# Parked operands written out one per neighbourhood head and fetched in the order of use, the last neighbourhood head with both score pairs first, and the two halves of a key block copied in one go

## The chip, the cores and the metric

The kernel runs on one core of a Trainium2 chip. The metric is the device time of one execution in microseconds (us); less is better. The kernel computes one denoising step of a small two-layer backbone. Three runs of the kernel before gave 1475.26, 1476.01 and 1476.55 us.

## The reference, cut to what matters

There are 512 latent tokens and 128 context ("prompt") tokens, so most operands are 640 columns wide, and 128 cached context tokens. Layer 0 mixes tokens by two kinds of heads, eight each; layer 1 by grouped-query attention; each layer ends in a SwiGLU feed-forward block. The change is in the mixer of layer 0:

```python
def even_mixer_latent(h, c_ckv, c_krope, c_nk, c_nv, w_in, q_norm, w_uq, kv_norm, w_ukv, rpb, w_out, cos, sin):
    q, ckv, krope, nq, nk, nv = even_project(h, w_in, q_norm, w_uq, kv_norm, w_ukv)
    q = jnp.concatenate([q[..., :MLA_NOPE_DIM], apply_rope(q[..., MLA_NOPE_DIM:], cos, sin)], axis=-1)
    krope = apply_rope(krope[:, :, None, :], cos, sin)[:, :, 0, :]
    k_lat, v_lat = mla_expand(ckv, w_ukv, krope)          # keys and values out of the 256-wide ckv
    k_ctx, v_ctx = mla_expand(c_ckv, w_ukv, c_krope)      # the same for the cached context
    a_mla = attend_blocked(q, cat(k_lat, k_ctx), cat(v_lat, v_ctx), MLA_SCALE)
    a_na = neighbourhood_attention(nq, nk, nv, c_nk, c_nv, rpb)
    return jnp.concatenate([a_mla, a_na], axis=-1) @ w_out
```

The MLA heads use `cq` (the 256-wide compressed query), `ckv` (256 wide) and `krope` (a rotary key of 32). All of it is computed in float32.

## The kernel before

**Arithmetic.** A float32 product is emulated on TensorE: each operand is split into a high part (`...h`, rounded to the fp32r type) and a low part (`...l`, the rest), and three matmuls (high by high, low by high, high by low) are added. A split costs two instructions: a copy on ScalarE (ACT) that makes the high part, and a subtraction on VectorE (DVE) that makes the low one. Weights arrive by DMA as float32 in one of a few `raw` buffers (`load`) and are split by `unit`, for the weights `wm0` to `wm3` with the subtraction on GpSimd (POOL).

**Stages.** After the input projection (which leaves `ckv`, `cq` and `kr`, the rotary key, unsplit on the chip) come the neighbourhood heads 0 to 7 ("NA"), from 113 to 218 us, then the MLA heads, then the output projection and the rest. Only the NA heads and the MLA heads are touched by the change.

**Parking.** The buffers that hold the split `ckv`, `cq` and `kr` for MLA are not free while NA runs. So `park` splits an operand in temporary buffers (three buffers of 640 columns, `tmp`, tiles `pt...h` and `pt...l`) and writes both parts to DRAM (tiles `pk...`). `latents`, `unpark` and `k_rope` fetch them back: `ck`, `ckp` (columns 512 to 640 and the cached context), `cq0`, `cq1` and the rotary rows of the key tiles `kT`. All these DMAs are issued from one queue, SyncE (SP), which also issues the loads of the weights and of the tables `gt` and `tq`. There are five parking steps, one written ahead of each of the heads 1 to 5 (`PARK_AT`).

**What sets the order.** The program lists its pieces by hand: `sequence` runs the pieces of a head in the order of a string. The strings for the heads 1 to 7 are in `NA_ORDER`: `s0`, `s1` are the two pairs of score blocks, `sp` the prompt's scores, `t0` to `t2` transposes and `v0` to `v2` the weighted values of the head before (the head's tail), `pt` and `pv` the same for the prompt, `q..` projection pieces of the next pair of heads, `m..` pieces of the modulation (weights `mraw`, `mraww`), and in head 7 `k0`, `k1` the first key block of MLA and `u0`, `u1` its first query. A second string orders the tail of head 7 beside the first two value blocks of MLA, `b0` and `b1`. The scheduler that builds the program places the instructions of the other engines into their queues; `tc.issue_after(x)` tells it that what is written inside stands behind `x`, but only on the engine of `x`. Each piece is issued after the last TensorE instruction before it, and so is a parking step by `after(PE.last, ...)`: this orders TensorE and nothing on ACT, DVE or SP, where the queue alone counts. Every engine works off its own queue strictly in order.

**Keys and queries of MLA.** `k_pieces` makes the key block of a pair of heads in two pieces: `mk..0` (512 columns) and `mk..1` (256). When a piece's matmuls are done, `k_set` copies it into the tiles of the even head (partitions 0 to 63, `kT..`) and of the odd head (64 to 127, `kT..` or `kTo`), once per head: ACT makes the high part, DVE the low part. `q_pieces` multiplies a query by a rotary table on DVE (`mqt`, table `tq0` for head 0 and `tq` for the others), and splits it. `mla_w(p)` loads and splits the weight `wm{p}`. `half_sum` adds the two halves of an attention result (ACT copies the upper half to `nhs` or `mhs`, DVE adds into `oN`).

Of the kernel before, what the change touches and what calls it, by code (L numbers as in the profile page):

```python
# [51 lines left out]
def body(ctx, tc, xT, vecs, crow, wm0, wm0g1, wm0g, wm1, wA, wNV, wNA, wMK, wMV, wOA, wGQ, wGK, wGV, wOC,  # L52
# [108 lines left out]


    def load(src, n, name):
        raw = rawp.tile([P, 1024], F32, tag="raw", name=name)
        nc.sync.dma_start(raw[:, :n], src)
        return raw[:, :n]

    def unit(src, n, name, lo="v", pool=None, bufs=3):
# [5 lines left out]
        (V if lo == "v" else G).tensor_tensor(lw, raw, f(hi), ALU.subtract)
# [236 lines left out]
    def half_sum(dsts, ps, n, pool, name):  # L411

        t = pool.tile([64, 512], F32, tag="hs", bufs=1, name=name)
        S.activation(t[:, :n], ps[64:128, :n], AF.Copy)
        for dst, a, b in dsts:
            V.tensor_tensor(dst, ps[0:64, a:b], t[:, a:b], ALU.add)
# [364 lines left out]
    def na_scores(h, bm, pts):  # L781
# [5 lines left out]
        def piece(jj):  # L787
            banks = [bank(f"ns{h}_{jj}{i}", "y") for i in range(2)]
            for j in (2 * jj, 2 * jj + 1):
                pss = banks[j % 2]  # L790
                k0, cq = P * PLACE[j][0], slice(P * j, P * j + P)
                PE.matmul(pss[:, 0:384], qh[:, cq], ks[:, k0:k0 + 384], start=True, stop=False)
                PE.matmul(pss[:, 0:384], ql[:, cq], ks[:, k0:k0 + 384], start=False, stop=True)
            for j in (2 * jj, 2 * jj + 1):
# [1 line left out]
                V.tensor_tensor_reduce(pt, banks[j % 2][:, :384], bm[:, (0, 1, 1, 2)[j], :], -1.0, 3.0e38, ALU.add, ALU.min,
                                       mm[:, j:j + 1])
# [90 lines left out]

    def k_set(r, rows, parts, src, p=0):

        jobs = []
        for c in parts:
            c0, c1 = KPART[c]
            o = c0 - KPART[parts[0]][0]
            h, l = [(prompt if c == 2 else main_[:, c0:c1])[rows] for main_, prompt in k_tiles(r, p)]
            jobs.append((h, l, src[rows, o:o + c1 - c0]))
# [1244 lines left out]
```

## Time and profile before

| | |
|---|---|
| runs | 1475.26, 1476.01, 1476.55 us; median 1476.01 |
| the profiled execution | 1476.62 us; its span 1474.5 us, so 2.12 us lie around it |
| TensorE (PE) busy | 1440.1 us, 98% of the span |
| VectorE (DVE), ScalarE (ACT), GpSimd (POOL) busy | 1231.4, 783.3, 175.0 us |
| granted TensorE clock | 0.996 |

All times inside an execution are counted from the start of the span. A row of the timeline gives start, duration, engine, line, operation, output and inputs, and in brackets how long the engine stood idle before it and what it waited for. Tile names have lost their numbers there, so `ns` is a score block of any NA head, `ms` of an MLA head, `mo` an MLA head's value product, `mts_0l` the low part of the transposed probabilities.

### The profile page before, as it was taken

To read this page: it belongs to the slowest core of one execution; us is meant where nothing else is said; L and a number is where in the kernel's file an instruction comes from. 1 tells how busy PE (TensorE), PEld (TensorE's weight loads), DVE (VectorE), ACT (ScalarE), POOL (GpSimd) and SP (SyncE) were. 2 spreads that over 40 slices of the span, in tenths; PEclk is the share of its full clock that TensorE was granted. 3 is DMA by queue.
4 is the path that set the end of the run, shared out by engine and by line. 5 is a ranking of instruction groups with operands and counts; after the bars stand their busy time and mean duration, and the time that the engine had idled before them with its cause. 6 is when DMAs were issued, how large, how long until landed. Compare 5 with 4: busy or idle time off the path is not lost.

```text
span 1474.5 us, 25877 instructions
## 1 busy us (share of the span) xinstructions
PE 1440.1 (98%) x9764; PEld 1390.1 (94%) x9764; DVE 1231.4 (84%) x2350; ACT 783.3 (53%) x1530; POOL 175.0 (12%) x270
## 2 busy tenths in 40 slices
PE   5999999999999999999999999999999999999997
PEld 4988888889999999999999999989999999999997
DVE  5877668877898989965997888888899898989976
ACT  5446667763755555541122666672656555555443
POOL 0037545430000000000000122220000000000000
PEclk9999999999999999999999999999999999999999
DMA  9655471026165555569764310115245555548572
GB/s 369 211 185 194 135 243 46 15 73 200 47 202 173 168 168 170 173 223 326 241 220 155 101 34 30 43 37 194 84 169 178 184 174 185 174 147 294 185 270 72
DMA packets 84884, 239.22 MB, mean 162 GB/s; under 512 B 9496, under 2 KB 15800, under 8 KB 84376
## 3 DMA queue, kind: packets, MB, share of 16 engines
q1 hardware_dynamic: 82400, 233.16, 47.2%
q10 hardware_dynamic: 1944, 3.48, 0.7%
q8 instruction: 76, 1.25, 0.4%
q0 software_dynamic: 416, 0.93, 0.2%
q14 instruction: 48, 0.39, 0.1%
HBM read 197.21 MB, written 40.33 MB: 161 GB/s over the span
## 4 chain that ended last, share of the span: by engine, by line
PE 83%; DVE 7%; ACT 4%; DMA 3%; issue 2%; DVEq 0%; ACTq 0%; POOL 0%; SPq 0%
PE fg L64 19%; PE fd L64 9%; PE fgo L64 5%; PE fo L64 5%; PE fu L64 4%; PE gq L64 3%; PE fdo L64 2%; PE gs L64 2%; PE go L64 2%; PE nk L64 1%; PE fuo L64 1%; DMA mraw<-in_wm 1%; PE gt L68 1%; PE mod L64 1%; ACT mp L1036 1%
## 5 line engine op out<-in xcount | busy, mean ns | idle before, releaser
L1708 DVE SCALAR_TENSOR_TENSOR junk<-wm,cb 128x1024 bf16<-128x1024 f32 x88 | 107.4, 1220 | 4.6 <-DMA wm<-in_wm 3.7
L64 PE MATMUL gq<-h10h,wgq 128*128 128x320 f32 x256 | 65.8, 316 | 0.0
L267 POOL TENSOR_SCALAR h10h<-h10t,gs,mods 128x320 fp32r<-128x320 f32 x4 | 3.9, 990 | 430.1 <-DVE h10t L261 427.7
L1448 ACT ACTIVATE wY<-s 128x1024 fp32r<-128x1024 f32 x38 | 40.3, 1061 | 27.4 <-PE fg L64 22.5
L1448 ACT ACTIVATE wZ<-s 128x1024 fp32r<-128x1024 f32 x38 | 40.2, 1057 | 21.1 <-PE fd L64 16.0
L1976 POOL TENSOR_TENSOR xr<-xw,fn1rs 128x320 f32<-128x320 f32 x2 | 1.7, 861 | 412.8 <-ACT fn1rs L235 412.8
L1449 DVE TENSOR_TENSOR wZ<-s,wZ 128x1024 fp32r<-128x1024 f32 x38 | 46.4, 1222 | 2.5
L1449 DVE TENSOR_TENSOR wY<-s,wY 128x1024 fp32r<-128x1024 f32 x38 | 46.3, 1220 | 0.3
L64 PEld LDWEIGHTS gq<-h10h,wgq 128*128 128x128 f32 x256 | 44.9, 189 | 0.6
L1557 DVE TENSOR_TENSOR sg<-up,sg 128x640 f32<-128x640 f32 x38 | 31.3, 823 | 15.9 <-ACT sg L1556 14.9
L1556 ACT ACTIVATE sg<-fg 128x320 f32<-128x320 f32 x38 | 16.7, 438 | 48.4 <-PE fg L64 48.4
L1578 ACT ACTIVATE p<-fd 128x320 f32<-128x320 f32 x38 | 16.6, 437 | 46.3 <-PE fd L64 46.3
L64 PE MATMUL gq<-h10l,wgq 128*128 128x320 f32 x128 | 39.4, 308 | 0.0
L1913 ACT ACTIVATE gp<-gs,gb,rq 128x640 f32<-128x640 f32 (+1 forms) x40 | 31.8, 796 | 13.2 <-DVE gb L1912 11.8
L64 PE MATMUL fg<-h01E,wW 128*128 128x320 f32 x228 | 36.6, 309 | 0.7 <-DVE g L1588 0.7
L64 PE MATMUL fg<-h01N,wZ 128*128 128x320 f32 x228 | 36.6, 309 | 0.5 <-ACT p L1576 0.5
L64 PE MATMUL fg<-h11N,wZ 128*128 128x320 f32 x228 | 36.7, 309 | 0.0
L64 PE MATMUL fg<-h01q,wX 128*128 128x320 f32 x228 | 36.7, 309 | 0.0
L64 PE MATMUL fu<-h11q,wX 128*128 128x320 f32 x228 | 36.6, 309 | 0.0
L64 PE MATMUL fd<-h01q,wZ 128*128 128x320 f32 x228 | 36.6, 309 | 0.0
L64 PE MATMUL fd<-h11q,wZ 128*128 128x320 f32 x228 | 36.6, 309 | 0.0
L64 PE MATMUL fg<-h11q,wX 128*128 128x320 f32 x228 | 36.5, 309 | 0.0
(3416 smaller groups left out, 5296.0 us busy)
## 6 DMA issues: line engine op xcount, KB each, us to landing
wm<-in_wm SPq DMA_DIRECT2D x48, 512.0 KB, 4.3
mraw<-in_wm SPq DMA_DIRECT2D x8, 1024.0 KB, 13.1
mraw<-in_wm SPq DMA_DIRECT2D x14, 512.0 KB, 4.3
wmv<-in_wm0g SPq DMA_DIRECT2D x8, 512.0 KB, 4.1
wm<-in_wm0g SPq DMA_DIRECT2D x8, 512.0 KB, 4.7
ruo<-in_wFO SPq DMA_DIRECT2D x8, 512.0 KB, 4.3
rgo<-in_wFO SPq DMA_DIRECT2D x8, 512.0 KB, 5.5
x<-in_xT SPq DMA_DIRECT2D x8, 320.0 KB, 5.6
```

What stands on the lines that cost most here:

```text
L64: cls.last = nc.tensor.matmul(*a, **k)
L68: cls.last = nc.tensor.transpose(*a, **k)
L267: G.tensor_scalar(h[:, c0:c1], t, self.gsl[:, k, 0:1], self.ml[:, self.sh + k, 0:1], ALU.mult, ALU.add)
L1036: exps[h, j] = S.activation(halves(pt), pss[:, :, :HT], AF.Exp, bias=nm, accum_out=ll[:, j:j + 1])
L1448: S.activation(h, src, AF.Copy)
L1449: V.tensor_tensor(w_, src, f(h), ALU.subtract)
L1556: last = S.activation(sg[:, 0:HT], g[:, :HT], AF.Silu, scale=-1.0)
L1557: V.tensor_tensor(sg, up, sg, ALU.mult)
L1578: S.activation(p5, b5[:, :HT], AF.Copy)
L1708: V.scalar_tensor_tensor(junk, raw, 1.0, cb[:, c, :], ALU.mult, ALU.mult, accum_out=mods[l][:, j0 + i, c:c + 1])
L1913: gexp[h, j] = S.activation(dst, src, AF.Exp, bias=nb, scale=rq[:, j:j + 1], accum_out=ll[:, j:j + 1])
L1976: G.tensor_tensor(x[k][:, c0:c1], root[1][k], nrm.rs[:, c0:c1], ALU.mult)
```

## The change

Seven edits, by the diff below.

1. Parking step h is now held behind the last exponential of head h - 1 (`nexps[h - 1, 3]`, an ACT instruction), on ACT's queue. So step 1 (`ckv0`) falls late into head 0's string, step 2 (`ckv1` and the cached context) into head 1's, step 3 (`cq0`) into head 2's, step 4 (`cq1`) into head 3's and step 5 (`kr`) into head 4's.
2. The fetches are put in the order of use on SP's queue: `latents` is held behind the load of `wm0`, the fetches of `cq` behind the load of `wmv`, the rotary rows behind the fetch of `cq1`.
3. Head 7 runs `s1` directly behind `s0`.
4. The split of `wmv` (`unit`) is cut from its load and held behind the last exponential of head 7.
5. In the tail of head 7 `b0` and `b1` stand ahead of `pt`.
6. `wm1`'s split is held behind `nhs7` (`done_with[7]`), the last ACT instruction that the values of head 7 need.
7. `k_set` copies both heads' halves in one go: all copies on ACT, then all subtractions on DVE.

```diff
-        nc.sync.dma_start(raw[:, :n], src)
+        fetched[name] = nc.sync.dma_start(raw[:, :n], src)
...
-    def unit(src, n, name, lo="v", pool=None, bufs=3):
+    def unit(src, n, name, lo="v", pool=None, bufs=3, raw=None):
-        raw = load(src, n, name + "r")
+        raw = load(src, n, name + "r") if raw is None else raw
...
-            wmk[p] = unit(wMK[p], 768, f"wm{p}", lo="g")
+            wmk[p] = after(done_with[7] if p == 1 else None, lambda: unit(wMK[p], 768, f"wm{p}", lo="g"))
...
-    def latents():
+    def latents(held):
+        with tc.issue_after(held.ins):
+            return latents_()
...
-    def k_set(r, rows, parts, src, p=0):
+    def k_set(parts, src, p):
         jobs = []
-        for c in parts:
...
+        for r in range(2):
+            rows = slice(64 * r, 64 * r + 64)
+            for c in parts:
...
         for h, l, part in jobs:
             S.activation(h, part, AF.Copy)
         for h, l, part in jobs:
             V.tensor_tensor(l, part, f(h), ALU.subtract)
...
-                for r in range(2):
-                    k_set(r, slice(64 * r, 64 * r + 64), parts, ps, p)
+                k_set(parts, ps, p)
...
-    NA_ORDER += ["s0 t0 t1 pt s1 m0 v0 t2 sp m1 v1 pv m2 v2", "s0 t0 t1 k0 s1 v0 t2 sp k1 v1 u0 v2 u1"]
+    NA_ORDER += ["s0 t0 t1 pt s1 m0 v0 t2 sp m1 v1 pv m2 v2", "s0 s1 t0 t1 k0 v0 t2 sp k1 v1 u0 v2 u1"]
...
-            after(PE.last, PARK_AT[h])
+            after(nexps[h - 1, 3], PARK_AT[h])
...
-            cqs = after(PE.last, lambda: [unpark(f"cq{u}") for u in range(2)])
+            cqs = after(fetched["wmvr"], lambda: [unpark(f"cq{u}") for u in range(2)])
...
-            lat = latents()
+            lat = latents(fetched["wm0r"])
...
-            wmv = unit(wMV, 1024, "wmv")
+            wmvr = load(wMV, 1024, "wmvr")
         if h == 7:
-            for r in range(2):
-                k_rope(r, (slice(64, 128), slice(0, 64))[r])
+            wmv = after(nexps[7, 3], lambda: unit(None, 1024, "wmv", raw=wmvr))
+            with tc.issue_after(fetched["cq1"].ins):
+                for r in range(2):
+                    k_rope(r, (slice(64, 128), slice(0, 64))[r])
...
-    sequence("t0 t1 t2 pt b0 b1 v0 v1 v2 pv", {**tail, ...})
+    sequence("t0 t1 t2 b0 b1 pt v0 v1 v2 pv", {**tail, ...})
```

**ACT at the start of NA.** `nqh` and `nk` are the high parts of the first heads' queries and keys; `np` are the exponentials of head 0. Before:

```order
L852 ACTIVATE ptckv10h<-ckvr_753 128x640
L724 ACTIVATE nqh_1021<-nq_1032 64x256
L724 ACTIVATE nqh_1022<-nq_1032 64x256
L724 ACTIVATE nqh_1021<-nq_1065 64x192
L173 ACTIVATE wnk_1191<-wnk1r 128x1024
L724 ACTIVATE nqh_1022<-nq_1065 64x192
L852 ACTIVATE ptcq00h<-cqr_594 128x640
L724 ACTIVATE nqh_1021<-nq_1065 64x128
L753 ACTIVATE nk_1030<-nk_1102 64x256
L852 ACTIVATE ptcq10h<-cqr_599 128x640
L724 ACTIVATE nqh_1022<-nq_1065 64x128
L753 ACTIVATE nk_1031<-nk_1102 64x256
```

And now, from the same copy of `nqh` on:

```order
L727 ACTIVATE nqh_1021<-nq_1032 64x256
L727 ACTIVATE nqh_1022<-nq_1032 64x256
L727 ACTIVATE nqh_1021<-nq_1065 64x192
L175 ACTIVATE wnk_1191<-wnk1r 128x1024
L727 ACTIVATE nqh_1022<-nq_1065 64x192
L727 ACTIVATE nqh_1021<-nq_1065 64x128
L756 ACTIVATE nk_1030<-nk_1102 64x256
L727 ACTIVATE nqh_1022<-nq_1065 64x128
L756 ACTIVATE nk_1031<-nk_1102 64x256
L747 ACTIVATE nkf_1162<-nk_1137 128x128
```

The copies for `ckv1`, `cq0` and `cq1` (`ptckv10h`, `ptcq00h`, `ptcq10h`) no longer stand among the copies of the first queries and keys.

**DVE late in head 2's string, around 146 us.** `nql` are low parts of the queries of heads 4 and 5, `oN` the sum of head 1's values, `npp0ptl` the low part of the first pair's transposed prompt probabilities. Before:

```order
L392 RECIPROCAL nr_3r<-nl_1548 128x1
L725 SCALAR_TENSOR_TENSOR nql_1564<-nq_1584,nqh_1562 64x64
L725 SCALAR_TENSOR_TENSOR nql_1565<-nq_1584,nqh_1563 64x64
L725 SCALAR_TENSOR_TENSOR nql_1564<-nq_1584,nqh_1562 64x256
L725 SCALAR_TENSOR_TENSOR nql_1565<-nq_1584,nqh_1563 64x256
L416 TENSOR_TENSOR oN_1177<-no_1639,nhs_1698 64x448
L416 TENSOR_TENSOR oN_1177<-no_1639,nhs_1698 64x64
L392 RECIPROCAL npp1r0r<-npp1l_1656 128x1
L405 TENSOR_TENSOR npp0ptl<-npp0t,npp0pth 128x256
```

And now:

```order
L394 RECIPROCAL nr_3r<-nl_1548 128x1
L728 SCALAR_TENSOR_TENSOR nql_1564<-nq_1584,nqh_1562 64x64
L856 TENSOR_TENSOR ptcq00l<-cqr_594,ptcq00h 128x640
L728 SCALAR_TENSOR_TENSOR nql_1565<-nq_1584,nqh_1563 64x64
L728 SCALAR_TENSOR_TENSOR nql_1564<-nq_1584,nqh_1562 64x256
L728 SCALAR_TENSOR_TENSOR nql_1565<-nq_1584,nqh_1563 64x256
L418 TENSOR_TENSOR oN_1177<-no_1639,nhs_1698 64x448
L418 TENSOR_TENSOR oN_1177<-no_1639,nhs_1698 64x64
L394 RECIPROCAL npp1r0r<-npp1l_1656 128x1
L407 TENSOR_TENSOR npp0ptl<-npp0t,npp0pth 128x256
```

The subtraction that parks `cq0` stands between the first two of the four `nql`; its copy stands at the same place on ACT.

**SP, the fetches of the last two heads.** `ck`, `cq` are the parked operands, `mraw_01_2450` and `wm0r` weights that head 6 and `k0` use. Before:

```order
L165 DMA mraw_00_2448<-in_wm 128x1024
L869 DMA ckl_2529<-pkckv0l 128x512
L869 DMA ckh_2527<-pkckv0h 128x512
L869 DMA ckh_2528<-pkckv1h 128x512
L869 DMA ckl_2530<-pkckv1l 128x512
L880 DMA cq0h<-pkcq0h 128x640
L880 DMA cq0l<-pkcq0l 128x640
L880 DMA cq1h<-pkcq1h 128x640
L165 DMA mraw_01_2450<-in_wm 128x1024
L165 DMA wm0r<-in_wMK 128x768
```

And now:

```order
L167 DMA mraw_00_2448<-in_wm 128x1024
L167 DMA mraw_01_2450<-in_wm 128x1024
L167 DMA wm0r<-in_wMK 128x768
L876 DMA ckh_2527<-pkckv0h 128x512
L876 DMA ckl_2529<-pkckv0l 128x512
L876 DMA ckh_2528<-pkckv1h 128x512
L876 DMA ckl_2530<-pkckv1l 128x512
L880 DMA ckph<-pkckv0h 128x128
L880 DMA ckph<-pkckv1h 128x128
L881 DMA ckph<-pkcch 128x2x128
```

The four `ck` and three of the `cq` went from ahead of the two weights to behind them; `cq` now follows behind the `ckp` rows and `wmvr`, and the `kT` rows follow `cq` as before.

**DVE in MLA head 1, at the second key block.** `kTl` is the low part of the even head's keys, `kTol` of the odd head's. Before:

```order
L392 RECIPROCAL mr_1r<-ml_2948 128x1
L900 TENSOR_TENSOR kTl_2545<-mk_2995,kTh_2543 64x512
L405 TENSOR_TENSOR mts_0l<-mt_0_3006,mts_0h 128x512
L405 TENSOR_TENSOR mts_1l<-mt_1_3015,mts_1h 128x512
L900 TENSOR_TENSOR kTol<-mk_2995,kToh 64x512
L928 TENSOR_TENSOR mqt_3031<-mq_3024,tq 128x320
```

And now:

```order
L394 RECIPROCAL mr_1r<-ml_2948 128x1
L909 TENSOR_TENSOR kTl_2545<-mk_2995,kTh_2543 64x512
L909 TENSOR_TENSOR kTol<-mk_2995,kToh 64x512
L407 TENSOR_TENSOR mts_0l<-mt_0_3006,mts_0h 128x512
L407 TENSOR_TENSOR mts_1l<-mt_1_3015,mts_1h 128x512
L936 TENSOR_TENSOR mqt_3031<-mq_3024,tq 128x320
```

`kTol` moved ahead of the two low parts `mts` of the transposed probabilities; the same happens at the key blocks in MLA heads 3 and 5, and likewise to the copies on ACT.

More of the change, by code (lines that the diff above doesn't have):

```diff
@@ L413, in half_sum @@
         t = pool.tile([64, 512], F32, tag="hs", bufs=1, name=name)
-        S.activation(t[:, :n], ps[64:128, :n], AF.Copy)
+        copied = S.activation(t[:, :n], ps[64:128, :n], AF.Copy)
         for dst, a, b in dsts:
             V.tensor_tensor(dst, ps[0:64, a:b], t[:, a:b], ALU.add)
+        return copied
     def scores(pss, q, kh, kl):
@@ L702, in body @@
     qbanks = [qbank, lambda name: bank(name, "y")]
-    nqk, wnas = {}, {}
+    nqk, wnas, done_with = {}, {}, {}
     def wna(p, i):
@@ L797, in piece @@
                                        mm[:, j:j + 1])
-                S.activation(pt, pt, AF.Exp, bias=mm[:, j:j + 1], scale=-1.0, accum_out=ll[:, j:j + 1])
+                nexps[h, j] = S.activation(pt, pt, AF.Exp, bias=mm[:, j:j + 1], scale=-1.0, accum_out=ll[:, j:j + 1])
                 softmax_tail(pt, ll[:, j:j + 1], f"nr{h}_{j}", 384)
@@ L829, in run @@
                 if n == 2:
-                    half_sum(((o[rr, 64:NS], 0, 448), (o[rr, 0:64], 448, NS)), box["o"], NS, ab, f"nhs{h}")
+                    done_with[h] = half_sum(((o[rr, 64:NS], 0, 448), (o[rr, 0:64], 448, NS)), box["o"], NS, ab, f"nhs{h}")
             return run
         return {**{f"t{n}": trs(n) for n in range(3)}, **{f"v{n}": av(n) for n in range(3)}}
-    wmk = {}
+    wmk, nexps = {}, {}
     def mla_w(p):
         if p not in wmk:
-            wmk[p] = unit(wMK[p], 768, f"wm{p}", lo="g")
+            wmk[p] = after(done_with[7] if p == 1 else None, lambda: unit(wMK[p], 768, f"wm{p}", lo="g"))
         return wmk[p]
@@ L862, in body, with latents_ @@
                3: lambda: park("cq0", cq[0], T), 4: lambda: park("cq1", cq[1], T), 5: lambda: park("kr", kr, 768)}
-    def latents():
+    def latents(held):
+        with tc.issue_after(held.ins):
+            return latents_()
+    def latents_():
         far = [[ring.tile([P, T], F32R, tag="h" + c, name=f"ck{c}{u}") for u in range(2)] for c in "hl"]
@@ L879, in unpark @@
         for t, d in zip(out, parked[name]):
-            nc.sync.dma_start(f(t), d)
+            fetched[name] = nc.sync.dma_start(f(t), d)
         return out
@@ L887, in k_tiles @@
         return odd_keys[p % 2] if r else even_keys
-    def k_set(r, rows, parts, src, p=0):
+    def k_set(parts, src, p):
         jobs = []
-        for c in parts:
[L893 to L896, printed above, removed]
+        for r in range(2):
+            rows = slice(64 * r, 64 * r + 64)
+            for c in parts:
+                c0, c1 = KPART[c]
+                o = c0 - KPART[parts[0]][0]
+                h, l = [(prompt if c == 2 else main_[:, c0:c1])[rows] for main_, prompt in k_tiles(r, p)]
+                jobs.append((h, l, src[rows, o:o + c1 - c0]))
         for h, l, part in jobs:
@@ L1000, in mv_early @@
         mvb[i] = mv_of(i, ybank)
-    sequence("t0 t1 t2 pt b0 b1 v0 v1 v2 pv", {**tail, **{f"b{i}": lambda i=i: mv_early(i) for i in range(6) if f"b{i}" in "t0 t1 t2 pt b0 b1 v0 v1 v2 pv"}})
+    sequence("t0 t1 t2 b0 b1 pt v0 v1 v2 pv", {**tail, **{f"b{i}": lambda i=i: mv_early(i) for i in range(6) if f"b{i}" in "t0 t1 t2 b0 b1 pt v0 v1 v2 pv"}})
     sb.close()
```

1 line of the change is left out of this document (added).

## The prediction

> **What bounds the kernel now.** I read the page's first part, then the waits, then the timelines at each place that the change touches.
>
> ```profile
> PE 1440.1 (98%) x9764; PEld 1390.1 (94%) x9764; DVE 1231.4 (84%) x2350; ACT 783.3 (53%) x1530; POOL 175.0 (12%) x270
> ```
>
> PE is the bound. The change takes no matmul away, so all it can win is time in which PE stands still, in the stretch that it touches. The view of waits, for PE from 95 to 330 us (total, times, longest), lists them.
>
> ```profile
> PE ms L64 <- ACT mp L1036: 2.3, 3, 0.9
> PE ns L64 <- DVE nk L754: 1.6, 1, 1.6
> PE mo L64 <- DVE mts_0l L405: 1.5, 3, 1.1
> PE npp3t L68 <- DVE oN L416: 0.9, 1, 0.9
> PE mk L64 <- DVE nm L796: 0.6, 1, 0.6
> PE no L64 <- DVE nts_0l L405: 0.4, 1, 0.4
> PE npp0o L64 <- DVE npp0ptl L405: 0.3, 1, 0.3
> PE mod L64 <- DMA mraw<-in_wm: 0.3, 1, 0.3
> ```
>
> That is 7.9 us in all. The first row lies inside MLA and nothing in the change shortens it. The change aims at the second (start of NA), the fourth to sixth (head 7) and the last; it adds work just ahead of the third and the seventh. Below, times are those of the profile before, and a term is what the end moves by.
>
> **Start of NA: minus 2.7.** The timelines of PE, ACT and DVE there:
>
> ```profile
> 113.05 0.31 PE L64 MATMUL nq<-h00h,wnq 128*128 128x320 f32 x1
> 115.87 0.44 PE L64 MATMUL ns<-nk,nqh 128*128 128x384 f32 x1 [1.62 <-DVE nk L754]
> 116.32 0.31 PE L64 MATMUL nq<-h00h,wnq 128*128 128x320 f32 x1
> 116.47 0.31 PE L64 MATMUL nq<-h00l,wnq 128*128 128x320 f32 x1
> 117.20 0.34 PE L64 MATMUL ns<-nk,nqh 128*128 128x384 f32 x1
> 117.38 0.34 PE L64 MATMUL ns<-nk,nql 128*128 128x384 f32 x1
> 118.59 0.36 PE L64 MATMUL nq<-h00h,wnq 128*128 128x320 f32 x1
> ...
> 106.68 0.74 ACT L852 ACTIVATE ptckv10h<-ckvr 128x640 fp32r<-128x640 f32 x1 [3.93 <-DMA out_o_nv<-nvf]
> ...
> 114.15 1.08 DVE L853 TENSOR_TENSOR ptcq10l<-cqr,ptcq10h 128x640 fp32r<-128x640 f32 x1
> ```
>
> ACT stood 3.93 us at a parking copy that waited for a temporary buffer, with all the query copies behind it; from then on ACT and DVE are late, and the `nk` for which PE waits stands behind the parking subtraction `ptcq10l`. All five steps leave this place. How much PE gets: the row alone says 1.6, the low end. The high end comes from pitches: between the starts at 113.05 and 118.59 lie seven `nq` (0.15 apart), eight `ns` (0.18) and two short prompt scores (0.13 each), about 2.7 us of work in 5.54, so 2.8. I take 2.7, near the high end, since ACT and DVE get back more than that: ACT three copies and the 3.93, DVE three subtractions.
>
> **One step per head: plus 1.35.** Each 640-column step is one ACT copy (0.74, the row above) and one DVE subtraction (1.08 above), and two DMAs on SP that block no load that is near its use. What it costs depends on what stands behind it:
>
> ```profile
> 125.00:137.00 12.00, 12.00 (x101) 10.28 (x99) 8.03 (x22) 7.70 (x22) 9.90 (x19) 1.00 0.47 155
> 163.84 0.55 DVE L754 TENSOR_TENSOR nk<-nk,nk 64x384 fp32r<-64x384 f32 x1 [1.55 <-ACT nk L753]
> 146.22 0.22 ACT L724 ACTIVATE nqh<-nq 64x64 fp32r<-64x64 f32 x1 [0.30 <-DVE nql L725]
> 149.70 0.42 DVE L405 TENSOR_TENSOR npp0ptl<-npp0t,npp0pth 128x256 fp32r<-128x256 f32 x1
> 173.70 0.22 ACT L724 ACTIVATE nqh<-nq 64x64 fp32r<-64x64 f32 x1 [0.78 <-DVE nql L725]
> ```
>
> Steps 1, 2 and 4: nothing. Step 1's work lies ahead of the stretch of the first row (columns: length, then busy time of PE, PEld, DVE, ACT), in which PE is full and DVE has 4 us in hand. Step 4, and step 2 in the same way, is covered by the 1.55 us in which DVE stands before the `nk` of 163.84; that cover gone, the `nk` behind it would be late by up to 0.8. Step 3 has no cover: from 145.7 to 149.7 ACT and DVE hand the four `nqh`/`nql` to and fro with gaps of 0.3 to 0.5, and at the end of that chain stands `npp0ptl`, for which PE waits already (0.3). The copy goes into one gap, the subtraction lands behind it: plus 0.9 (0 to 1.2). Step 5 meets the same chain two heads on, but there ACT stands 0.78 anyway: plus 0.45 (0 to 0.8).
>
> **Fetches in the order of use: minus 0.35.** Head 6's `mraw` competes with seven fetches that were issued just before it:
>
> ```profile
> 191.19 4.91 DMA mraw<-in_wm
> mraw<-in_wm SPq DMA_DIRECT2D x14, 512.0 KB, 4.3
> 190.00:200.00 10.00, 9.71 (x95) 6.86 (x94) 7.05 (x23) 7.44 (x20) 3.60 (x5) 1.00 1.02 367
> cq1l<-pkcq1l SPq DMA_DIRECT2D x1, 320.0 KB, 5.8
> 200.08 0.60 SPq L905 DMA_DIRECT2D kTl<-pkkrl  x1
> 209.29 0.31 PE L64 MATMUL mq<-cq1l,wm 128*128 128x320 f32 x1
> ```
>
> At the median of its group it lands 0.6 sooner, and PE waits 0.3, so between 0 and 0.6. The fetches are later by 5 us or more: `cq1l` becomes the sixteenth transfer behind `mraw`; at 0.6 per issue it leaves at about 200.8 and lands 5.8 later, at 206.6. PE used it at 209.3, and by the next part will at 208.4: covered by 1.8 us. That cover gone, `q`'s multiplication in head 7 waits, us for us.
>
> **Head 7 and its tail: minus 1.2.** The split of `wmv` (1.22 on DVE, at 202.65) stands ahead of the tail's `nts_0l` and leaves that place, which takes the 0.4; with `s1` early, `k1` has its PSUM bank in time, which takes the 0.6. So the transposes at 210.95 come about 0.9 sooner.
>
> ```profile
> 202.65 1.22 DVE L174 TENSOR_TENSOR wmv<-wmvr,wmv 128x1024 fp32r<-128x1024 f32 x1
> 211.46 0.49 DVE L928 TENSOR_TENSOR mqt<-mq,tq 128x320 f32<-128x320 f32 x1
> 213.47 0.71 PE L64 MATMUL mv<-wmv,ckh 128*128 128x512 f32 x2
> ```
>
> Then the 0.9 at `npp3t` goes too, but another wait takes its place: `b0`'s second matmul needs the low part of `wmv`, which now stands behind the last `mqt`. That ends at 211.95 less 0.9, and 1.22 more makes 212.3, where before that matmul ran at 213.7: 1.4 sooner, less 0.2 for `pt`, which now comes behind `b1`. Ends: 0.5, if DVE is later by a sum or two, and 1.6.
>
> **The table for MLA: plus 0.3.** Before, `wm1` was split by 213.4; now its ACT copy waits for `nhs`, and POOL's part follows. A weight load (`oaw0r`) waits on SP for the buffer, and the table `tq` is queued behind it.
>
> ```profile
> 218.12 0.59 ACT L414 ACTIVATE nhs<-no 64x512 f32<-64x512 f32 x1 [0.99 <-PE no L64]
> 211.62 1.82 POOL L174 TENSOR_TENSOR wm<-wm1r,wm 128x768 fp32r<-128x768 f32 x1 [0.68 <-PE nt L68]
> tq<-in_tabM SPq DMA_DIRECT2D x1, 640.0 KB, 6.3
> 226.00 0.48 DVE L928 TENSOR_TENSOR mqt<-mq,tq 128x320 f32<-128x320 f32 x1
> ```
>
> With `nhs` at 218.12 less 1.2, 0.6 for it, about 0.8 for the copy and 1.82 on POOL, `tq` is issued at 220.6 and lands by 6.3 at 226.9; DVE comes to the `mqt` that reads it at 224.8. So DVE stands 2.1 there, and a maximum and an exponential of head 0 stand behind. But that 6.3 was taken beside two other weight loads; now there is one, and 512 KB land in 4.3 by the median above. So it lands after 4.3 to 6.3, and DVE stands 0.1 to 2.1, of which about 1 is hidden, since PE has one more score block to do before it needs that exponential's bank. I take 0.3, range 0 to 2. Here the Trainium skill, "SBUF — State Buffer", section "The DMA setup-cost knee", speaks for less: about 2 us and the bytes at 436 GB/s, so 3.5 us here by an estimate from that page, and no stall; the row's 6.3 disagrees, and the term would be 0 instead of 0.3.
>
> **Key halves in one go: plus 0.9.** The two halves lie in one PSUM bank.
>
> ```profile
> 236.59 0.58 ACT L898 ACTIVATE kTh<-mk 64x512 fp32r<-64x512 f32 x1
> 237.20 0.68 DVE L900 TENSOR_TENSOR kTl<-mk,kTh 64x512 fp32r<-64x512 f32 x1 [0.25 <-ACT kTh L898]
> 286.46 0.67 DVE L900 TENSOR_TENSOR kTl<-mk,kTh 64x512 fp32r<-64x512 f32 x1
> 287.17 0.59 ACT L898 ACTIVATE kToh<-mk 64x512 fp32r<-64x512 f32 x1 [0.47 <-DVE kTl L900]
> ```
>
> The last row shows ACT's second copy waiting for DVE's first subtraction: the program keeps two engines off one bank. So now the first subtraction waits for both copies, 0.48 later (the pitch of two such copies), and PE's `mo`, which waits for the second DVE instruction here before and after, comes 0.45 later in heads 1 and 3. In head 5 DVE arrives late at 286.46 anyway: nothing. Together 0.9, between 0 (the work behind it absorbs it) and 1.4. The Trainium skill, "PSUM — Partial Sum Buffer", section "PSUM bank collisions raise a hardware error", says that two engines collide only in the same bank and 32-partition quadrant; the halves lie in different ones, so by it the wait need not be. The row shows that it is there. Without it this term would be 0 and the sum lower by 0.9.
>
> **Sum.** -2.7 + 0.9 + 0.45 - 0.35 - 1.2 + 0.3 + 0.9 = -1.7 us. The profiled execution took 1476.62 (span 1474.5 and 2.12 around it) and becomes 1474.9; it stands 0.61 above the median, 1476.01, from which I get 1474.3. All terms at their good ends give -5.05, all at their bad ends +3.3. A difference under 0.2%, 2.95 us, can hardly be told from none by this measurement.
>
> **Rivals.**
> - *The added work is hidden.* Steps 3 and 5 and the key halves cost nothing: -2.7 - 0.35 - 1.2 + 0.3 = -3.95, 1472.1, faster. For it: DVE's 84%. Against it: PE waits already at all those places. 0.25.
> - *The table is the new bound.* `tq` lands after 6.3 or more and all of the stall reaches PE: +2 instead of +0.3, sum 0, 1476.0. For it: the queue order. Against: fewer loads beside it. 0.10.
> - *The fetches come too late, slower.* They share SP's queue and the DMA engines, which stood at 1.02 of their share with 367 GB/s. Each us that `cq1l` lands after 208.4 is lost. Up to it 4.3 MB go (by the shapes in the queue); at half the 367 that takes 23.4 us from 191.2, to 214.6: +6.2 on the sum, 1480.5. A landing at 210.1 (228 GB/s) cancels the gain, one at 213.1 (197 GB/s) makes the kernel slower by over 0.2%. Against it: the 367. 0.08.
> - *The steps do not really move*: if the hold binds less than the text says, the start stays as it is and no step is added later: -0.35 - 1.2 + 0.3 + 0.9, 1475.7. The queue order as built speaks against. 0.03.
>
> **Chances.** The forecast itself, between -2.95 and +0.5: 0.54. Faster by over 0.2%: the first rival and a little of the forecast's tail, 0.27; slower: the third, 0.08; within: 0.65. The range reaches from 1471.8 (the first rival) to 1477.0 (the table late and step 3 at its worst).
>
> **What would show it.** Right: PE goes through 113 to 119 without the wait at `ns`; the wait at `npp0o` grows from 0.3 to about 1.2; `npp3t`, `mk` and `no` leave the list in head 7 and `mv` waits for DVE's `wmv` about 1 us; `mo` waits about 0.8 in MLA head 1; DVE stands at the first `mqt` of MLA for `tq`. Wrong: a wait at `mq` for `cq` in head 7, a wait at `ms` of over 1 us at 225 to 232, or `ns` still waiting for `nk`.

## The result and the profile after

The changed kernel is slower: 1481.85 us (median of six runs, 1480.09 to 1483.32) against 1475.7 us for the kernel before on the same chip (six runs). The ratio is 1.0036, 95% interval 1.0022 to 1.005; it is that of the means, while the medians lie 6.15 us apart, since one of the six executions of before took 1480.39. The forecast was 1474.3, with "within 0.2%" the likeliest outcome and 1477.0 the upper end.

The profiled execution of after took 1481.18 us, its span 1479.3, so 4.8 more than the span before. The page's first part and the view of waits for PE from 90 to 340 us (total, times, longest):

```profile
PE 1440.8 (97%) x9764; PEld 1390.1 (94%) x9764; DVE 1229.5 (83%) x2350; ACT 782.2 (53%) x1530; POOL 176.4 (12%) x270
```

```profile
PE ms L64 <- ACT mp L1046: 3.9, 5, 1.3
PE no L64 <- ACT nts_0h L403: 2.7, 1, 2.7
PE mo L64 <- DVE kTol L909: 2.1, 2, 1.2
PE mo L64 <- DVE kTl L909: 0.8, 1, 0.8
PE mv L64 <- DVE wmv L176: 0.7, 1, 0.7
PE mk L64 <- DVE mts_0l L407: 0.5, 3, 0.2
```

PE does the same matmuls for the same busy time. Gone from the list before are `ns` (1.6), `npp3t` (0.9) and `mod` (0.3); new are `no` waiting 2.7 for ACT in head 2, `mo` waiting for the key halves, and `mv` waiting for `wmv`.

To see where time goes, I take the start of the same matmul in two profiled executions and subtract; the change of this shift over a stretch is what the stretch lost (+) or won. Ends of the stretches by the time before: 111.4, 138.3 (first value block of head 0 done), 152.8 (head 2), 196.7 (start of head 7), 216.3 (its tail), 232.2 (first MLA head), 306.3 (last key block), 691.5. The first column is there ahead of any changed instruction, -0.7 to -2.0 against this execution of before. It arises between 23 and 31 us: there this execution ran at half its clock, from 22.46 to 29.28, and of the others only run 10 did, for 3.41 us. So it says nothing of the change.

| kernel | ahead | start of NA | head 2 | heads 3 to 6 | head 7 | table | MLA keys | rest | end |
|---|---|---|---|---|---|---|---|---|---|
| after | -1.55 | -2.58 | +5.82 | -0.18 | -0.57 | +0.50 | +4.09 | -0.80 | +4.73 |
| 1 copy of wnq3 later | -1.14 | -2.58 | +3.17 | -0.16 | 0.00 | +0.62 | +4.05 | -0.68 | +3.28 |
| 2 keys apart | -1.99 | -2.58 | +7.11 | +0.44 | -0.67 | +0.89 | +0.02 | +2.07 | +5.29 |
| 3 keys only | -1.66 | +0.94 | +0.51 | +0.05 | -1.24 | 0.00 | +4.32 | -0.62 | +2.30 |
| 4 parks only | -1.11 | -2.59 | +5.04 | +0.38 | 0.00 | +0.01 | -0.01 | -0.38 | +1.34 |
| 5 steps moved | -1.09 | -2.58 | +0.22 | -0.51 | +1.75 | +0.90 | -0.30 | -0.48 | -2.09 |
| 6 table sooner | -1.14 | -2.58 | +0.36 | -0.49 | +1.52 | +0.09 | -0.09 | +0.30 | -2.03 |
| 7 weight last | -1.13 | -2.58 | +0.10 | -0.50 | +1.70 | +0.09 | -0.04 | +0.04 | -2.32 |
| 8 filled wait | -2.00 | -2.58 | +5.89 | -0.18 | -0.42 | +0.60 | +4.03 | -0.98 | +4.36 |
| 9 both cuts | -0.74 | -2.58 | +3.10 | -0.05 | -0.67 | +0.89 | 0.00 | +1.07 | +1.02 |
| 10 query sooner | -0.99 | -2.58 | +0.63 | -0.49 | -0.71 | +0.09 | -0.02 | -0.19 | -4.26 |

The first row is the result in short: the start of NA pays what was forecast, and head 2 (+5.82) and the MLA keys (+4.09) take back almost four times as much. Each row is one execution. Run 3 has +0.94 and +0.51 in two stretches in which its program is that of before, so a single figure of that size can be chance; figures that many rows share, like -2.58, are not. The verdicts go by the timed ratios.

**Head 2.** The timeline of ACT in after, and the row of before for the same weight (in the brackets: idle time before, and the releaser):

```profile
139.47 1.06 ACT L175 ACTIVATE wnq<-wnq3r 128x1024 fp32r<-128x1024 f32 x1 [5.19 <-DMA wnq3r<-in_wNA]
140.54 0.60 ACT L403 ACTIVATE nts_0h<-nt 128x512 fp32r<-128x512 f32 x1
```

```profile
139.10 1.06 ACT L173 ACTIVATE wnq<-wnq3r 128x1024 fp32r<-128x1024 f32 x1 [0.71 <-DMA wnq3r<-in_wNA]
```

ACT stands 5.19 us at the copy of a weight that has not landed. The weight is for heads 6 and 7, nobody needs it now; but `nts_0h`, for which PE waits, is the next instruction in ACT's queue. In before the same copy stood 0.71 at the same DMA: it had no slack there. Why the weight is late shows on SP and in the DMA issues from 130 to 145 us (last number: us from issue to landing), first after, then before:

```profile
132.34 0.58 SPq L858 DMA_DIRECT2D pkckv1h<-ptckv10h  x1
133.01 0.38 SPq L858 DMA_DIRECT2D pkckv1l<-ptckv10l  x1
133.49 0.41 SPq L167 DMA_DIRECT2D wnq3r<-in_wNA  x1
...
wnq3r<-in_wNA SPq DMA_DIRECT2D x1, 512.0 KB, 6.0
```

```profile
135.24 0.34 SPq L165 DMA_DIRECT2D wnq3r<-in_wNA  x1
...
wnq3r<-in_wNA SPq DMA_DIRECT2D x1, 512.0 KB, 3.8
```

The two writes of parking step 2 (320 KB each) now stand directly ahead of the load and move beside it, and it takes 6.0 instead of 3.8. In all ten kernels with these writes it takes 5.3 to 6.0, without them 3.8 (before) and 4.1 (run 3). PE is 4.1 us sooner at this place than before, while the load leaves only 1.75 sooner: the time won at the start shortens the time that this prefetch has. What holds its issue, as far as these rows show, is not the writes but the table `gt` ahead of them on SP. It waits for POOL, and left only 1.87 sooner (131.73, before 133.60); the load follows `gt` by 1.76 here and by 1.64 in before. SP's waits from 125 to 138 us, after and before (L774 and L771 are the lines of `gt`):

```profile
SPq L774 <- POOL np L395: 8.7, 1, 8.7
```

```profile
SPq L771 <- POOL np L393: 6.4, 1, 6.4
```

PE then, and the windows of after (columns: length, busy time of PE, PEld, DVE, ACT, POOL, granted clock, DMA share, GB/s):

```profile
141.19 0.80 PE L64 MATMUL no<-nts_0h,nv 128*128 128x512 f32 x1 [2.68 <-ACT nts_0h L403]
```

```profile
137.25:140.66 3.41, 1.26 (x8) 0.94 (x7) 0.00 (x0) 1.17 (x2) 0.00 (x0) 1.00 0.98 347
140.66:144.07 3.41, 2.88 (x10) 2.25 (x11) 2.52 (x5) 2.56 (x7) 1.43 (x2) 0.50 0.38 143
144.07:147.48 3.41, 3.41 (x15) 3.41 (x15) 2.86 (x11) 2.45 (x8) 3.30 (x8) 0.50 0.52 156
147.48:150.89 3.41, 3.41 (x27) 3.41 (x27) 2.09 (x6) 1.61 (x4) 1.30 (x2) 1.00 0.67 201
```

After the wait PE runs at half its clock for 6.8 us (15 matmuls in a window instead of 27). It is busy for 2.88 and 3.41 of them, so it loses about 3.1 us. 2.68 and 3.1 make 5.8, and the table has +5.82; run 2 below shows that the two are not independent.

**MLA keys.** ACT, DVE and PE at the second key block in MLA head 1, after:

```profile
237.74 0.58 ACT L907 ACTIVATE kTh<-mk 64x512 fp32r<-64x512 f32 x1
238.33 0.60 ACT L907 ACTIVATE kToh<-mk 64x512 fp32r<-64x512 f32 x1
...
238.96 0.68 DVE L909 TENSOR_TENSOR kTl<-mk,kTh 64x512 fp32r<-64x512 f32 x1 [0.85 <-ACT kToh L907]
239.66 0.69 DVE L909 TENSOR_TENSOR kTol<-mk,kToh 64x512 fp32r<-64x512 f32 x1
...
240.50 0.46 PE L64 MATMUL mo<-mts_0h,mv 128*128 128x512 f32 x1 [0.90 <-DVE kTol L909]
```

The first subtraction starts 1.22 behind the start of `kTh` (0.61 before, from 236.59 to 237.20) and the second 0.70 later; the `mts` low parts and DVE's row maximum stand behind both, where before they stood between.

**Head 7.** SP and PE, with the DMA issue of `cq1l`:

```profile
203.61 0.43 SPq L887 DMA_DIRECT2D cq1l<-pkcq1l  x1
...
cq1l<-pkcq1l SPq DMA_DIRECT2D x1, 320.0 KB, 5.4
...
209.97 0.31 PE L64 MATMUL mq<-cq1l,wm 128*128 128x320 f32 x1
214.47 0.50 PE L64 MATMUL mv<-wmv,ckh 128*128 128x512 f32 x1 [0.74 <-DVE wmv L176]
```

`cq1l` lands at 209.0, 1.0 us ahead of its use, with PE late by 0.7 at this place (209.97, before 209.29).

### The profile page after: what moved, and what is told of

Same layout as the page of the kernel before. It is cut to its first block, busy times and chain, and to the rows that moved or that the text cites. A ratio compares the mean times of both kernels' runs of the same rounds, so it can differ in the third digit from the quotient of the medians.

```text
span 1479.3 us, 25872 instructions
## 1 busy us (share of the span) xinstructions
PE 1440.8 (97%) x9764; PEld 1390.1 (94%) x9764; DVE 1229.5 (83%) x2350; ACT 782.2 (53%) x1530; POOL 176.4 (12%) x270
## 4 chain that ended last, share of the span: by engine, by line
PE 86%; DVE 6%; ACT 4%; issue 2%; DMA 1%; POOL 0%; DVEq 0%; ACTq 0%; SPq 0%; POOLq 0%
PE fg L64 20%; PE fd L64 9%; PE fgo L64 5%; PE fo L64 5%; PE fu L64 4%; PE gq L64 3%; PE fdo L64 2%; PE nk L64 2%; PE gs L64 2%; PE go L64 2%; PE fuo L64 1%; PE nq L64 1%; PE mod L64 1%; PE gt L68 1%; PE gvp L64 1%
## 5 line engine op out<-in xcount | busy, mean ns | idle before, releaser
L64 PE MATMUL fg<-h11E,wW 128*128 128x320 f32 x228 | 36.5, 309 | 0.0
```

What stands on the lines that cost most here:

```text
L64: cls.last = nc.tensor.matmul(*a, **k)
```

## The experiments

Every expectation stands as it was written before its run. Ratios are to the kernel before on the same chip, with 95% intervals. In some of them the word "held" is used of a load; `after(x, ...)` with an ACT instruction holds only what stands on ACT, so it is the weight's copy that moved, and the DMA stayed at its place on SP.

**1. The copy of wnq3 behind head 2's first exponentials**, all else as after:

```diff
+                held = nexps[2, 1] if (p_, i_) == (3, 0) else None
-                wnas[p_, i_] = unit(wNA[p_, i_], 1024, ...)
+                wnas[p_, i_] = after(held, lambda: unit(wNA[p_, i_], 1024, ...))
```

> The changed kernel with one hold added: the split of the weight wnq3 (used two heads later) stands behind the second exponential of head 2 instead of ahead of nts_0h. Theory A (the loss comes from ACT standing at this copy until its DMA lands, with PE's nts_0h behind it, and from PE's clock, granted at half for some 6 us after PE has stood 2.7 us): the wait at no<-nts_0h goes (under 0.5 us), the granted clock stays at 1.00 from 137 to 150, and about 2.7 + 3.3 = 6 us come back: about 1.5 us above before, 1477.2 on a before of 1475.7. Rival B (the half clock comes from elsewhere, the power of the denser start of NA, and would come anyway): the wait goes but the clock still falls near 140, only 2.7 come back, 1479. Rival C (the parking DMAs saturate the chip's transfers and something else waits as long): no gain, 1481.

Measured: 1.001 (0.9998 to 1.0022), so 1.5 us above before, as theory A said: about 3.8 of the 5.3 us that the ratio 1.0036 stands for are gone. Its clock is off, though: that still fell, only later (148.35). The wait at `no` is gone, though the weight is issued at 134.24 and lands no sooner: `nts_0h` now stands ahead of the copy. (The scheduler also moved `nts_2h` and step 3's copy by a few places, to 142.18 and 142.66.) ACT in this run:

```profile
136.13 0.60 ACT L403 ACTIVATE nts_0h<-nt 128x512 fp32r<-128x512 f32 x1 [1.45 <-PE nt L68]
...
140.02 1.06 ACT L175 ACTIVATE wnq<-wnq3r 128x1024 fp32r<-128x1024 f32 x1 [1.39 <-DMA wnq3r<-in_wNA]
```

But head 2 still loses 3.17. With PE in time at `no`, parking step 3 shows its price, first the wait, then two windows:

```profile
PE npp0o L64 <- ACT npp0pth L403: 1.5, 1, 1.5
```

```profile
144.83:148.24 3.41, 1.69 (x12) 1.29 (x10) 2.30 (x7) 2.29 (x7) 0.37 (x1) 1.00 0.89 351
148.24:151.65 3.41, 3.41 (x16) 3.41 (x17) 2.44 (x10) 1.96 (x6) 1.80 (x3) 0.52 0.02 7
```

A wait of 1.5 and 1.7 us of clock. In after that wait isn't there, since PE, slowed, comes late itself. Not every execution need pay this: of the twelve, four took 1481.86 us or more at a granted clock of 0.995 or 0.996, the eight others at most 1479.89 at 0.997 or 0.998.

**2. Key halves copied per head as before**, all else as after (the loop over the heads back around `k_set`):

> The changed kernel with the two halves of a key block copied one after the other again, as before (also in head 7); all else as changed. Theory A: by the shifts of PE's landmarks MLA lost about 4 us between 232 and 306, at mo (0.9, 0.8, 1.2 of wait) and at ms, and this comes back, less up to 0.5 in head 7: about 4 us under the changed kernel, 1477.7, with the waits of mo back to 0.3, 0.1 and 1.0. Rival B (the MLA losses come from the late table tq and the late exponentials behind it, not from the key halves): the mo waits change but the end moves by under 1.5 us, 1480.5.

Measured: 1.0008 (0.9999 to 1.0017). The MLA keys lose +0.02 instead of +4.09, so the seventh edit alone costs about 4 us. Up to head 7 the program is the same as in after. The `no` wait is there (2.3), but here the clock stays full behind it, and now PE has to wait at `npp0o`:

```profile
149.90 0.44 PE L64 MATMUL npp0o<-npp0pth,nv 128*128 128x128 f32 x1 [1.86 <-ACT npp0pth L403]
```

Up to this matmul head 2 has lost 4.9 at full clock, so from late data alone; then the clock falls (149.96).

**3. Key halves in one go as the only change to before:**

```diff
-                for r in range(2):
-                    k_set(r, slice(64 * r, 64 * r + 64), parts, ps, p)
+                k_set(parts, ps, p)
```

> The kernel before with only the key halves copied in one go. Theory A: about 4 us slower than before in MLA (heads 1, 3, 5: some 1.3 us each), within 0.5 us of that after what head 7 gains or loses: 1479.5. Rival B: what the prediction had, plus 0.9: 1476.6. Rival C (in head 7 it gains as much as it loses in MLA): 1475.7.

Measured: 1.0013 (1.0004 to 1.0023). The MLA keys lose +4.32, head 7 wins 1.24. The loss is this edit's own and needs nothing of the others; in head 7 the same edit helps. By the time alone it is about 1.9 us (0.6 to 3.4): theory A's 1479.5 (3.8) lies above the interval, since head 7 wins more than the 0.5 that it allowed, and rival B's 0.9 lies in it. It is the trace that settles where the 4 us are.

**4. Parking behind the exponentials as the only change to before** (`after(nexps[h - 1, 3], PARK_AT[h])`):

> The kernel before with only the parking steps held, one per head. Theory A: the start of NA gains 2.4 us as in the changed kernel, then ACT stands at the copy of wnq3, PE waits about 2.7 us at no<-nts_0h and runs at a granted clock near 0.5 for some 6 us, costing 6: about 3.6 us slower than before, 1479.3. Rival B (the wait arises only together with the other edits): no wait there, 2 us faster than before, 1473.7.

Measured: 1.0008 (0.9999 to 1.0017). Start -2.59, head 2 +5.04: the parking steps' new places by themselves win and lose both. Both theories miss the time (theory A 3.6 slower, rival B 2 faster, measured about 1.2 slower). Theory A's wait is there: PE waits 2.5 at `no` for `nts_0h`; but one window behind it is slow, not two:

```profile
138.11:141.52 3.41, 0.90 (x6) 0.58 (x5) 0.09 (x1) 1.77 (x3) 0.00 (x0) 0.99 0.88 328
141.52:144.93 3.41, 3.41 (x12) 2.79 (x13) 3.02 (x6) 2.15 (x6) 2.03 (x2) 0.51 0.39 140
```

**5. Steps moved, keys in one go only in head 7.** The copy of `wnq3` as in 1; `cq0` and `cq1` parked in head 3 (behind `nexps[3, 1]` and `nexps[3, 3]`), `kr` behind `nexps[5, 3]`:

```diff
-            after(nexps[h - 1, 3], PARK_AT[h])
+            for hh_, j_, step_ in PARK_AT.get(h, ()):
+                after(nexps[hh_, j_], step_)
...
-                k_set(parts, ps, p)
+                for heads in (((0, 1),) if p == 0 else ((0,), (1,))):
+                    k_set(heads, parts, ps, p)
```

> The changed kernel with three things altered: key halves in one go only in head 7, one after the other in MLA; steps 3 and 5 taken out of the even heads' strings (cq0 and cq1 behind exponentials of head 3, kr behind the last exponential of head 5); the split of wnq3 held behind the second exponential of head 2. Theory A (the three causes found are all there is): the start keeps its 2.4 us through head 6, no wait at no<-nts_0h, at npp0o no more than the 0.3 of before, granted clock 1.00 throughout, MLA as before apart from the table; end 3.5 to 4 us under before, ratio 0.9975. Rival B (the steps cost about 1 us wherever they stand): the gain of the start is gone by head 6, ratio 0.999 to 1.000.

Measured: 0.999 (0.9982 to 0.9999). Head 2 loses only 0.22 and the MLA keys nothing. Theory A's 0.9975 is outside the interval, and rival B, whose ratio fits, has the mechanism wrong: the gain is still there at the start of head 7, where PE comes 4 us sooner than before. There the fetches are late, and behind the waits the clock is halved from 206.42 to 209.83, which is 1.7 us more. So head 7 loses 1.75, although its own waits of before are gone:

```profile
PE mq L64 <- DMA cq1h<-pkcq1h: 0.8, 1, 0.8
PE mq L64 <- DMA cq1l<-pkcq1l: 0.5, 1, 0.5
```

**6. The table `tq` ahead of the weight load `oaw0r` on SP**, else as 5:

> As steps_moved, and the table tq is issued ahead of oaw0r, so that it no longer waits for the split of wm1. Theory A (the late table costs 0.5 to 0.9 us at the start of MLA): DVE no longer stands at the first mqt for tq, the landmarks between 216 and 232 us keep their distance, and 0.5 to 0.9 come back. Rival B (the exponentials are late because of the split of wm1 on ACT itself or of wm2): no change.

Measured: 0.9987 (0.9976 to 0.9997). The column "table" goes from +0.90 to +0.09, as theory A said; the two ratios are too close to show it. In after the table is issued when the weight ahead of it has its buffer; here 11 us sooner (SP and the DMA issue of after, the `mqt` that reads the table, and last SP of this run):

```profile
222.43 0.33 SPq L167 DMA_DIRECT2D oaw0r<-in_wOA  x1
222.85 0.38 SPq L1018 DMA_DIRECT2D tq<-in_tabM  x1
...
tq<-in_tabM SPq DMA_DIRECT2D x1, 640.0 KB, 4.8
...
227.75 0.49 DVE L936 TENSOR_TENSOR mqt<-mq,tq 128x320 f32<-128x320 f32 x1 [0.63 <-PE ms L64]
```

```profile
211.63 0.39 SPq L1021 DMA_DIRECT2D tq<-in_tabM  x1
```

The view puts DVE's 0.63 down to PE's `ms`, which this `mqt` doesn't read; 222.85 and 4.8 make 227.65, 0.1 ahead of the end of that wait: it was the table.

**7. The load of `wmv` behind the `cq` fetches**, else as 6:

> As table_sooner, and the load of wmv goes behind the fetches of cq instead of ahead of them. Theory A (with the start 2.4 us sooner, PE comes to cq1l before it has landed; in the run with wnq3 held it waited 0.8): the wait at mq for cq1l is there in steps_moved (0.5 to 1) and gone here, 0.5 to 0.8 sooner, if wmv is still in time for b0. Rival B (wmv now lands too late): a wait at mv of over 1 us takes its place.

Measured: 0.9979 (0.997 to 0.9989), 1473.25 us. `mq` still waits, once, 1.3 for `cq1l`, and `mv` 1.7 for `wmv`; head 7 loses as in 5 (+1.70). So theory A is wrong, and rival B's wait at `mv` has come beside the other.

**8. The wait filled:** after, with 14 idle matmuls on PE ahead of head 1's first value block (in head 2's string), where the wait of 2.7 stands; the value block overwrites what they write:

```diff
+                    if h == 1:
+                        for _ in range(14):
+                            PE.matmul(box["o"][:, 0:384], nqk[1][0][0][:, 0:P], nqk[1][2][0][:, 0:384], start=True, stop=True)
```

> The changed kernel with 14 idle matmuls (2.5 us of work whose result is overwritten) on PE where it waits for nts_0h in head 2; everything else as changed. Theory A (the clock is granted at half because PE stood still): the granted clock stays 1.00 from 137 to 150, the end is about 3 us sooner than the changed kernel although nothing is ready sooner, 1479. Rival B (the clock falls for another reason, or late data alone make the loss): the clock falls as before or the end stays, 1482.

Measured: 1.0056 (1.0041 to 1.0072). The granted clock stays at 1.00 from 137 to 150, so in head 2 it is PE standing still that halves it. But head 2 loses 5.89, as in after, and theory A's 3 us don't come. At full clock PE runs into ACT and DVE, which are late themselves:

```profile
146.40 0.50 PE L64 MATMUL no<-nts_2h,nv 128*128 128x256 f32 x2 [0.93 <-ACT nts_2h L403]
147.67 0.50 PE L64 MATMUL no<-nts_2l,nv 128*128 128x256 f32 x2 [0.77 <-DVE nts_2l L407]
150.96 0.33 PE L64 MATMUL npp0o<-npp0pth,nv 128*128 128x128 f32 x1 [0.80 <-ACT npp0pth L403]
```

But the idle matmuls changed more than PE. The scheduler placed `nts_2h` behind the parking of `cq0` here, while in after it stands ahead of it (143.67 and 146.18); ACT in this run:

```profile
145.14 0.72 ACT L858 ACTIVATE ptcq00h<-cqr 128x640 fp32r<-128x640 f32 x1
145.77 0.57 ACT L403 ACTIVATE nts_2h<-nt 128x512 fp32r<-128x512 f32 x1
```

So the waits at `nts_2h` and `nts_2l`, 1.7 together, may be this run's own. Run 2 is the cleaner witness: with after's order and the clock still full, late data alone cost 4.9, where after has 5.8 with half the clock. So in after the slow clock and the late data largely cover each other, and most of the loss in head 2 is late data. That this kernel is timed slower than after, though up to 691 us its profiled execution loses 0.4 less, stays unexplained; the two intervals overlap.

**9. Both cures at once,** 1 and 2:

> The changed kernel with the two cures together that were tried one at a time: wnq3's load held back by a head and a half, and the key halves copied head by head as before. Theory A (the late weight and the key halves are two separate losses, and they are all of it): the ratios of the changed kernel, 1.0036, and of the two single cures, 1.001 and 1.0008, add up: 1.0036 - 0.0026 - 0.0028 = 0.9982, about 1473.3 us beside a before of 1476; no wait at `no` in head 2, about 1.5 us at `npp0o`, MLA without loss. Rival B (they cover each other, since whichever comes first leaves the later one more slack): ratio 1.000 or above.

Measured: 0.9988 (0.9977 to 1.0), 1476.3 us against 1478.43. Theory A gave 0.9982: the two losses add up within the interval, whose upper end is rival B's 1.000, and with both gone the slowdown is gone. Step 3 still costs +3.10 in the profiled execution (1.5 of wait, 1.7 of clock). Its ratio equals that of 5, which moved step 3 away, so over many executions that price must be smaller than in this one, or 5 gives it back in head 7. The profiled executions show the second (head 7: +1.75 in 5, -0.67 here); the first isn't excluded.

**10. The `cq` fetches ahead of the six `ckp` fetches,** else as 7 (`rest` issues the six):

```diff
+            after(fetched["cq1"], fetched["rest"])
-            wmvr = after(fetched["cq1"], lambda: load(wMV, 1024, "wmvr"))
+            wmvr = after(fetched["ckp"], lambda: load(wMV, 1024, "wmvr"))
```

> The best version so far (weight wmvr last) with the four cq fetches ahead of the six ckp fetches. Theory A (cq1l is late only because it is issued as the fourteenth fetch; 2.9 us of issues go from ahead of it): the wait of 1.3 us at mq is gone, ckp is 2 us later but still in time for the second key piece, and the end moves by 0.5 to 1.3 us sooner: ratio about 0.9975. Rival B (the DMA engines are full there, so the order changes only who waits): mk waits for ckp, or mv longer for wmv (now 1.7), and the ratio stays at 0.998.

Measured: 0.9967 (0.9956 to 0.9978), 1473.01 us against 1478.43: faster than both kernels; theory A's 0.9975 lies in the interval, rival B's 0.998 just outside. The wait at `mq` is gone, that at `mv` too, and head 7 wins 0.71 instead of losing 1.70. Rival B's `mk` does wait for `ckp`, for less than what is won:

```profile
PE mk L64 <- DMA ckph<-pkcch: 0.4, 1, 0.4
PE mk L64 <- DMA ckpl<-pkccl: 0.4, 1, 0.4
```

## Why the prediction was wrong, term by term

**Start of NA, -2.7: right.** All ten kernels with the parking steps moved show -2.58 or -2.59. The `ns` blocks run without a wait (113.23, 113.40, 113.68, 113.93 in after), as the high end worked out from the pitches said.

**One step per head, +1.35: the step that failed.** "Steps 1, 2 and 4: nothing" was argued from the idle time of ACT and DVE; of SP the working said "two DMAs on SP that block no load that is near its use". Step 2's two writes stand directly ahead of `wnq3r`, and the load lands 6.0 instead of 3.8 after its issue. Its use isn't near for PE, but its copy is near on ACT's queue, and in front of work that is. The row at 139.10 of before, an idle time of 0.71 for that DMA, said that this prefetch had nothing in hand; the working doesn't use it. So "nothing" was +5.8. Runs 1, 4 and 5 show it: the same +5 with the parking alone, 3.2 once the copy stands behind `nts_0h`, and 0.2 when step 3 is taken out of this head too. The load lands 4.6 us later against PE than before: 2.2 of it are the longer flight beside the writes, and 2.4 are PE being 4.1 sooner while the issue, behind `gt`, moved only 1.75. By these rows the first is the step's own, and the second belongs to the gain at the start; no run changes one of the two alone.

Step 3, +0.9, was placed rightly (`npp0o`, where PE waits 1.7 in all in run 1 and 0.5 in run 5, which has the step elsewhere: 1.2, the upper end), but its price has a second part that no term had: 1.7 us of halved clock behind the wait. In after neither shows, since head 2's own lateness covers it. Step 5, +0.45: +0.3, since heads 3 to 6 come out at -0.18 in after and at -0.5 in runs 5, 6, 7 and 10, where it stands elsewhere.

**Order of the fetches, -0.35: right in the sum.** `mod` leaves the list, and those -0.5 are this term. The cover of 1.8 us at `cq1l` was 1.0, and gone as soon as PE is sooner: the waits for `cq` are 0.8 in run 1, 0.9 in 9 and 1.3 in 5, 6 and 7. So the third rival has its mechanism right, from the point at which the other losses are mended; the cure was to issue `cq` ahead of `ckp`.

**Head 7 and its tail, -1.2: half, near the low end of 0.5.** -0.57 in after, -0.67 without the key halves in one go (2 and 9). `npp3t` is gone and `mv` waits 0.74, as said. The key halves there, which the working gave no term, are worth -1.24 alone (run 3) and not in addition. Why only half came, no run separates.

**Table, +0.3:** +0.5 to +0.9, inside its 0 to 2. It landed 4.8 us after its issue, between the 4.3 and the 6.3 of the rows. By the Trainium skill, "SBUF — State Buffer", section "The DMA setup-cost knee", the estimate was 3.5; the trace disagrees here too, and by less than it seemed to from 6.3.

**Key halves, +0.9: the right place, mis-sized at a fifth.** Measured +4.1 (after), +4.3 alone, 0 without. Two things were short. The first subtraction is 0.61 later, not 0.48: two copies out of one bank follow each other at 0.59, without the overlap that the pitch taken for them has. In run 3 PE's `mo` comes 0.8 later in heads 1 and 3, where 0.45 was forecast, and 0.2 in head 5, where nothing was (it stands 1.24 at 292.46 in after, and stood 1.05 there before). And the price was made for `mo` alone, while `mts` and the row maxima behind both subtractions are late as well. In run 3 each of the three heads loses another 0.3 around the `mo` of `mts_2l` and 0.4 to 0.5 at an `ms` that waits for `mp`. That is 1.8 at the place forecast and 2.4 behind it, 4.2 of the 4.3. The Trainium skill, "PSUM — Partial Sum Buffer", section "PSUM bank collisions raise a hardware error", puts the two halves in different quadrants and so lets two engines at them; the 0.85 for which `kTl` waits for `kToh` shows again that this program keeps them apart.

In sum: -2.6 + 5.8 - 0.2 - 0.6 + 0.5 + 4.1 = +7.0 against -1.7 forecast, less 0.8 given back later and the 1.55 ahead, which makes the +4.7 of the profile. No rival had a copy held on ACT by a prefetched weight, and the range held neither of the two mis-sized terms. Of the signs named for a right forecast nearly all came true (`npp0o` is the exception), and the kernel is slower all the same: they were signs of the terms that were listed.

## What to carry to other kernels

Before work is put ahead of something on a queue, look for the prefetch behind it that already lands last (an idle time "<-DMA" on an engine that only splits or copies it), and ask what urgent work stands behind that copy in the same in-order queue; putting the copy behind the urgent work took away 3.8 us here. Time won early is kept only if each later supply, fetch and table is early by as much: here three in a row (`wnq3`, `cq`, `tq`) took it back until the copy was moved or they were issued sooner. Handing copies to ACT and subtractions to DVE in batches made the first of them wait for the whole batch here, where both halves lie in one bank, and everything behind it too.

## What the runs showed of the hardware

The granted clock was not on the list of costs. It halved behind waits of 1.5 to 2.7 us in head 2, but not behind the one of 2.3 in run 2. Every slow stretch inside an execution lasted 3.41 us (runs 1, 4, 5, 7, 9 and 10) or 6.83 (before, after and run 2). A slow piece of 3.41 us in which PE is busy throughout costs 1.7 us of work.

It is tempting to read a limit out of the pieces of 3.41 us ahead of the falls in head 2: PE is busy there for 0.90 (run 4), 1.26 (after), 1.55 (run 2) and 1.69 us (runs 1 and 9), at most half, and a piece of 1.76 in run 2 is not followed by a fall. The other traces don't bear it out. Two pieces of run 2, then two of run 5, the second of them followed by a slow piece at 865.20, and one of run 8:

```profile
136.31:139.72 3.41, 1.76 (x12) 1.44 (x10) 0.00 (x0) 1.06 (x2) 0.20 (x1) 1.00 0.92 332
146.55:149.96 3.41, 1.55 (x12) 1.28 (x10) 2.27 (x7) 2.20 (x7) 1.42 (x2) 1.00 0.63 182
203.01:206.42 3.41, 2.11 (x15) 1.56 (x13) 3.02 (x8) 2.88 (x9) 0.53 (x2) 1.00 1.03 371
861.78:865.19 3.41, 2.92 (x22) 2.39 (x20) 3.38 (x8) 1.71 (x5) 0.60 (x1) 1.00 0.22 48
19.96:23.37 3.41, 1.52 (x24) 0.78 (x28) 3.41 (x8) 1.32 (x4) 0.00 (x0) 1.00 1.02 410
```

The clock fell behind 2.11 and 2.92 (in run 7 behind 2.92 too, in before behind 1.99), and it did not fall behind the 1.52 of run 8. Nor does one figure end a slow stretch: a slow piece with PE busy for 3.05 was the last in run 10, while one with 3.31 was followed by a second in run 2. So the busy time of the view doesn't decide it, and what does stays open. The Trainium skill, "TensorE: Matmul & The Clock Gate", section "Part 1: The HAM clock gate", says that the window is 3413 ns long and runs free, and the lengths agree; it gives "≥1 idle window" for the fall, and there the measurement decides: PE was idle throughout none of the pieces ahead of these falls. If the borders run free, one execution of a kernel may pay and the next may not. The spread of before would fit that: of the 20 executions timed beside run 9, nine at a granted clock of 0.995 took 1479.25 us on average, and nine at 0.998 or 0.999 took 1476.74. That wasn't tried by itself.
